# A hybrid attention and recurrence block: ScalarE, VectorE and SyncE of the input projection in program order, with each split, store and gate a set number of products behind what it needs

## The chip, the cores and the metric

The kernel runs on one core of a Trainium2 chip. The metric is the device time of one launch in microseconds, less is better. The kernel before took 2325.84 us in the median of three runs (2323.38 to 2326.81). TensorE is the matmul engine, ScalarE and VectorE work on one element per lane and cycle streams, GpSimd does general work, and SyncE only starts transfers; GpSimd starts some too. Every engine has its own queue.

## The reference

One layer of a decoder on 2048 tokens of width 1024. A sandwich-normed mixer is followed by a sandwich-normed MLP of hidden width 4096. Cut to the mixer, in which the change lies:

```python
h = rms_norm(x, mix_norm_pre)
z = h @ w_in                                   # 1024 -> 2560
q, k, v, xr, gr = split(z)                     # 512 columns each
attn = dilated_attention(q, k, v)              # 8 heads of 64, windows 128, 512, 2048, dilations 1, 4, 16
xr   = causal_depthwise_conv(xr, conv_w, conv_b)               # 4 taps
r, i = sigmoid(blocks(xr) @ w_r + b_r), sigmoid(blocks(xr) @ w_i + b_i)
a    = exp(-8 * r * softplus(-lam))
state_t = a_t * state_{t-1} + sqrt(1 - a_t ** 2) * (i_t * xr_t)
m    = concat(attn, state * gelu(gr)) @ w_out
x    = x + rms_norm(m, mix_norm_post)          # then the MLP
```

## The kernel before

**Numbers.** A float32 operand is split into an upper part, rounded by a ScalarE copy, and a lower part, the rest, by a subtraction on VectorE or GpSimd (`split`, L50). A matmul of two such operands is three: upper by upper, lower by upper, upper by lower (L206 to L208).

**Tiles of the projection.** Weights of `w_in` come in 20 tiles of 128 columns: 4 each for q, k, v, x (the recurrence's input) and g (its gate). Tokens come in blocks of 512; two blocks are a half, and a half's two blocks are b = 0 and 1. One product (`product`) is one tile by one block: 8 steps of three matmuls into one bank of PSUM. Banks have tags: "P" two buffers (products), "X" one (transposes of v, gate matmuls `pr` and `pi`, norm spreads), the others for attention.

**Stages.** `begin` opens with the products of x0, g0, x1, g1 on half 0. Then `stream` runs through the list `JOBS`, tile by tile, with both blocks of a tile. After ten products' worth of steps (`AHEADJOBS`) `interleave` takes over: it writes the attention of half 0 and between its parts calls `fill(n)`, which lets `stream` go on by n steps. So the rest of half 0's tiles and all of half 1's are computed inside and behind the attention of half 0. After that come the output projection and MLP of half 0, with the attention of half 1 in between, and those of half 1.

**What follows a product.** q and k: an eviction with the norm factor (`zn`, L219, L221), a split into `zh`, `zl`, stores to DRAM (L228, L229). v: an eviction, four transposes on TensorE (L235), a split into `vs` (one buffer), one store (L239). x: `convolved` (eviction `xr` L374, taps L377 to L380), then `opened` 10 steps later: gate matmuls `pr` (L391) and `pi` (L398), tanh, exp, square, root, and the scan of the state (L411). g: `gated`, a tanh GELU, and at its end the product with the state (L437) and a store. Weight tiles are loaded one tile ahead (`load_w`, L104) and split at once. Blocks 2 and 3 of the input replace 0 and 1 in the middle of the list (`load_x`: one transfer, an upper part `hH` L166 and a lower part `hL` L167 for each of eight column tiles; `spread_norm`: the norm's factors spread to all partitions by a matmul `pbc` L186). `between` also starts copies of `w_out` and `w2` from DRAM to DRAM on GpSimd's queue (L1550).

**What sets the order.** A step calls `passed`, which runs what `after(n, fn)` put n steps later, so the program says how many steps behind its product a thing is written. In the projection and in the attention of half 0, though, only TensorE keeps the order of the program (`manual_schedule` with PE alone). The order of ScalarE, VectorE, GpSimd and SyncE is made by a scheduler from its own estimate of times. In the attention of half 1 the order of ScalarE, VectorE and SyncE is the program's too. In the join of the heads, `sa` (L729) is made on VectorE and `pst` (L736) reads it on TensorE after one `yield`, which is one fill.

Of the kernel before, what the change touches and what calls it, by code (L numbers as in the profile page):

```python
# [86 lines left out]
class Project:  # L87
# [9 lines left out]
    def load_w(self, hf, ct, lo_eng=None, px=None):  # L97
# [3 lines left out]
        for half in range(2):  # L101
# [3 lines left out]
            split(nc, hi[:, k0:k0 + KT // 2, :], lo[:, k0:k0 + KT // 2, :], raw, lo_eng=lo_eng or self.lo)  # L105
# [39 lines left out]
    def load_x(self, tb, px=None, also=None):  # L145
# [3 lines left out]
        row = []  # L149
        b = tb % NBH  # L150
        for k in range(KT):
# [5 lines left out]
            elif px:  # L157
                raw = px.tile([P, TB], F32, tag="xl", bufs=2, name=f"xr{tb}_{k}")
            else:
                raw = self.pa.tile([P, TB], F32, tag="wraw", bufs=2, name=f"xr{tb}_{k}")  # L160
            nc.sync.dma_start(out=raw, in_=self.xT[k, :, cs])
            if tb == 0 and k == 0:
                nc.sync.dma_start(out=self.g1, in_=self.g1_d)
            hi = p.tile([P, TB], F32R, tag="hH", bufs=2 * KT, name=f"hH{tb}_{k}")
            lo = p.tile([P, TB], F32R, tag=f"hL{b}_{k}", bufs=1, name=f"hL{tb}_{k}")
            nc.scalar.activation(out=hi, in_=raw, func=AF.Identity, scale=self.g1[:, k:k + 1])  # L166
            nc.vector.scalar_tensor_tensor(out=lo, in0=raw, scalar=self.g1[:, k:k + 1], in1=f32(hi),  # L167
                                           op0=ALU.mult, op1=ALU.subtract)
            row.append((hi, lo))
            if also:  # L170
                also(k)
        self.h[tb % NBH] = row

    def spread_norm(self, tb, px=None):
# [15 lines left out]
        for j in range(TB // P):  # L190
            if px:
                made(j)
                spread(j)
            else:
                self.after(4 + 3 * j, lambda j=j: made(j))
                self.after(6 + 3 * j, lambda j=j: spread(j))
# [14 lines left out]
    def stored(self, kind, hf, pr, b, z):  # L211
# [10 lines left out]
        if kind != "v":  # L222
            zh = self.pa.tile([P, TB], F32R, tag="zh", bufs=1, name=f"zh{n}")
            zl = self.pa.tile([P, TB], F32R, tag="zl", bufs=1, name=f"zl{n}")
            self.cst["pool"] = split(nc, zh, zl, zn, lo_eng=self.lo)[1]
            dst = scr[kind][hf][pr]
            for u in range(2):
                nc.sync.dma_start(out=f32(dst[u, 0, :, cs]), in_=f32(zh[u * HD:(u + 1) * HD, :]))  # L228
                nc.sync.dma_start(out=f32(dst[u, 1, :, cs]), in_=f32(zl[u * HD:(u + 1) * HD, :]))  # L229
            return  # L230

        def turned():
            pt = self.bank("X", f"vt{n}")
            for j in range(TB // P):
# [3 lines left out]
            split(nc, vs[:, :, :, 0, :], vs[:, :, :, 1, :], ptv)  # L238
            nc.sync.dma_start(out=f32(scr["v"][hf][pr][cs, :].rearrange("(n p) c -> p n c", p=P)),  # L239
                              in_=f32(vs.rearrange("p n u a c -> p n (u a c)")))  # L240

        self.after(4, turned)

    def after(self, n, fn):

        self.due.append([n, fn])

# [8 lines left out]
    def stream(self, jobs, between):  # L256
# [5 lines left out]
        loaded = {}  # L262
# [6 lines left out]
        load()  # L269
# [97 lines left out]
    def convolved(self, hf, c, b, zx, wait, px=None):  # L367
# [7 lines left out]
        s.copy(out=self.tail[:, c, :], in_=xr[:, TB:TB + 3])  # L375
# [1333 lines left out]
```

## Time and profile before

| what | value |
|---|---|
| median of the runs | 2325.84 us (2323.38 to 2326.81) |
| the profiled execution, and its span | 2326.59 us, 2324.7 us |
| mean granted TensorE clock | 0.982 |
| TensorE busy | 2191.8 us, 94% |
| opening: 0 to 90 us | TensorE busy 79.06 |
| stream alone: 90 to 250 us | TensorE busy 147.9 of 160 |
| attention of half 0 with the rest of the stream: 250 to 555 us | TensorE busy 278.89 of 305 |
| rest of the stream: 555 to 651 us | TensorE busy 92.83 of 96 |

The times are of one execution under the profiler. A row of the timeline reads: start, duration, engine, line, operation, output, inputs, count, and in square brackets how long the engine had been idle and what ended that. A window row reads: stretch, its length, busy time (and count) of TensorE, its weight loads, VectorE, ScalarE and GpSimd, then the granted clock, the share of the DMA engines and GB/s.

### The profile page before, as it was taken

How to read it: one execution, taken by the hardware profiler on the slowest of the kernel's cores; microseconds unless marked ns; L12 is line 12 of the kernel's file. 1: busy time of each engine (PE TensorE's matmuls, PEld its weight loads, DVE VectorE, ACT ScalarE, POOL GpSimd, SP SyncE). 2: the span in 40 equal slices, each digit the busy share in tenths (PEclk: the TensorE clock that was granted, in tenths of full speed). 3: DMA queues.
4: the chain of work that ended last, by engine and by line, in shares of the span. 5: the costliest groups of instructions: out<-in, count | busy, mean ns of one | idle time of the engine just before them, and what ended most of it. 6: DMA issues, size and time to landing. Idle time of an engine off the chain costs nothing.

```text
span 2324.7 us, 30774 instructions
## 1 busy us (share of the span) xinstructions
PE 2191.8 (94%) x10264; PEld 1778.9 (77%) x10264; DVE 1510.7 (65%) x3022; ACT 1268.2 (55%) x2569; POOL 404.5 (17%) x491
## 2 busy tenths in 40 slices
PE   8989899999999899998999999898999999999998
PEld 6668677777788677786777787677878888788887
DVE  6564677685448777774667676766775656455556
ACT  7654556675334545453656565755455555563543
POOL 3434413233014201001001011114200000000003
PEclk9999999999999999999999999999999999999999
DMA  8487574424744577868767777858455443586665
GB/s 287 140 238 238 195 219 131 136 78 119 244 150 162 202 274 262 307 236 269 229 193 211 204 226 205 220 173 262 152 180 186 150 150 143 211 279 191 194 195 181
DMA packets 217551, 466.15 MB, mean 201 GB/s; under 512 B 22464, under 2 KB 77152, under 8 KB 211120
## 3 DMA queue, kind: packets, MB, share of 16 engines
q1 hardware_dynamic: 188624, 329.52, 45.3%
q0 software_dynamic: 28768, 134.66, 16.3%
q8 instruction: 81, 1.33, 0.2%
q14 instruction: 78, 0.64, 0.1%
HBM read 329.75 MB, written 151.13 MB: 207 GB/s over the span
## 4 chain that ended last, share of the span: by engine, by line
PE 49%; DVE 12%; DMA 8%; ACT 7%; issue 6%; POOL 1%; SPq 0%; DVEq 0%; ACTq 0%; POOLq 0%
PE o L1220 6%; PE o L1221 5%; PE o L1219 5%; PE za L1080 4%; PE za L1081 4%; PE za L1082 4%; PE m L906 2%; PE m L904 2%; PE m L905 2%; PE zc L1080 2%; PE zc L1081 2%; PE zc L1082 2%; DMA w2s<-in_dram 2%; PE z L206 1%; PE z L207 1%
## 5 line engine op out<-in xcount | busy, mean ns | idle before, releaser
L206 PE MATMUL z<-hH,wH 128*128 128x512 f32 x640 | 272.8, 426 | 14.8 <-DVE xr L374 7.7
L207 PE MATMUL z<-hL,wH 128*128 128x512 f32 x640 | 256.3, 400 | 0.2 <-DVE hL L167 0.2
L208 PE MATMUL z<-hH,wL 128*128 128x512 f32 x640 | 254.9, 398 | 0.0
L206 PEld LDWEIGHTS z<-hH,wH 128*128 128x128 f32 x640 | 123.3, 193 | 42.8 <-issue 13.0
L207 PEld LDWEIGHTS z<-hL,wH 128*128 128x128 f32 x640 | 122.8, 192 | 28.1 <-issue 5.1
L208 PEld LDWEIGHTS z<-hH,wL 128*128 128x128 f32 x640 | 122.5, 191 | 28.1
L514 ACT ACTIVATE smB<-smB,negB 128x128 f32<-128x128 f32 (+3 forms) x128 | 71.5, 559 | 105.2 <-DVE negB L510 104.8
L55 POOL TENSOR_TENSOR wL<-wraw,wH 128x512 fp32r<-128x512 f32 x62 | 88.8, 1449 | 171.4 <-ACT wH L54 168.7
L1085 ACT ACTIVATE sq<-sq 128x512 f32<-128x512 f32 x93 | 58.9, 633 | 84.6 <-DVE sq L1089 84.6
L514 ACT ACTIVATE sm<-sm,neg 128x256 f32<-128x256 f32 (+1 forms) x128 | 63.2, 495 | 67.9 <-DVE neg L510 67.5
L1145 POOL DMA_DIRECT2D sa<-sq x31 | 16.5, 532 | 401.3 <-ACT sq L1086 400.9
L55 DVE TENSOR_TENSOR tlB<-pT_B,thB 128x384 fp32r<-128x384 f32 x96 | 57.3, 597 | 44.2 <-ACT thB L54 43.9
L1086 ACT ACTIVATE sq<-sq 128x512 f32<-128x512 f32 x124 | 76.7, 629 | 2.4
L503 DVE CUSTOM_DVE_ANT_0 smB<-SB,mask_b 128x128 f32<-128x128 f32 (+3 forms) x128 | 59.5, 483 | 25.5 <-PE SB L679 25.4
L54 ACT CAST wH<-wraw 128x512 fp32r<-128x512 f32 (+1 forms) x81 | 46.9, 610 | 35.6 <-PE z L207 21.3
L1156 DVE TENSOR_TENSOR w2s<-w2s 128x512 f32<-128x512 f32 x64 | 44.1, 689 | 32.5 <-DMA w2s<-in_dram 31.6
L704 PE MATMUL oB<-tlB,vb 128*128 128x256 f32 x192 | 47.0, 294 | 12.6 <-DVE tlB L55 10.7
L1080 PE MATMUL za<-hHT,f_6H 128*128 128x512 f32 x128 | 51.8, 405 | 7.3 <-ACT sq L1119 7.2
L1253 POOL TENSOR_TENSOR y<-y,g4b 128x512 f32<-128x512 f32 x8 | 13.0, 1658 | 261.0 <-ACT junk_y L84 261.0
L476 PE MATMUL pT_B<-ident,smB 128*128 128x128 f32 x320 | 52.3, 278 | 5.6 <-DVE nb L497 3.6
L55 DVE TENSOR_TENSOR tlA<-pT,thA 128x512 fp32r<-128x512 f32 (+1 forms) x64 | 42.8, 668 | 22.7 <-ACT thA L54 22.2
L54 ACT CAST thB<-pT_B 128x384 fp32r<-128x384 f32 x96 | 48.5, 505 | 12.6 <-PE pT_B L476 11.9
(573 smaller groups left out, 7059.3 us busy)
## 6 DMA issues: line engine op xcount, KB each, us to landing
sa<-as POOLq DMA_DIRECT2D x32, 1024.0 KB, 5.8
w1r<-in_dram SPq DMA_DIRECT2D x58, 512.0 KB, 4.0
sa<-sq POOLq DMA_DIRECT2D x31, 768.0 KB, 3.6
wraw<-in_dram SPq DMA_DIRECT2D x79, 256.0 KB, 3.3
w2s<-in_dram SPq DMA_DIRECT2D x16, 1024.0 KB, 7.4
sb<-w2s POOLq DMA_DIRECT2D x16, 1024.0 KB, 6.5
kh<-sk SPq DMA_DIRECT2D x24, 512.0 KB, 5.1
kl<-sk SPq DMA_DIRECT2D x24, 512.0 KB, 6.6
```

The source lines that it names most:

```text
L54: return (nc.scalar.copy(out=hi, in_=src), (lo_eng or nc.vector).tensor_tensor(out=lo, in0=src, in1=f32(hi), op=ALU.subtract))
L55: (lo_eng or nc.vector).tensor_tensor(out=lo, in0=src, in1=f32(hi), op=ALU.subtract))
L206: pe.matmul(z, hi[:, k, :], hh, start=(k == 0), stop=False)
L207: pe.matmul(z, hi[:, k, :], hl, start=False, stop=False)
L208: pe.matmul(z, lo[:, k, :], hh, start=False, stop=(k == KT - 1))
L514: s.activation(out=sm[:, c0:c0 + w], in_=sm[:, c0:c0 + w], func=AF.Exp, bias=neg[:, j:j + 1], accum_out=st[:, 1, u, cols[j]:cols[j] + 1])
L1080: pe.matmul(o, hi[:, k], bh[:, k], start=start and k == 0, stop=False, skip_group_check=True)
L1081: pe.matmul(o, hi[:, k], bl[:, k], start=False, stop=False, skip_group_check=True)
L1082: pe.matmul(o, lo[:, k], bh[:, k], start=False, stop=k == KH - 1, skip_group_check=True)
L1219: pe.matmul(o, ah[:, ts], bh, start=fresh and j == 0, stop=False, skip_group_check=True)
L1220: pe.matmul(o, ah[:, ts], bl, start=False, stop=False, skip_group_check=True)
L1221: pe.matmul(o, al[:, ts], bh, start=False, stop=j == NJ - 1, skip_group_check=True)
```

## The change

Around the projection and the attention of half 0, the order of ScalarE, VectorE and SyncE is now the program's as well (`ORDERED`); GpSimd stays with the scheduler. So that the program's order can serve, each thing that follows a product is put at a number of steps of its own:

- weight tiles: cast 8 and 9 steps behind the load, the lower part one step behind each cast (before: at once);
- q and k: split at 1 and 2, upper part stored at 2, lower at 4; v: transposes at 6 (before 4), split 1 and 2 steps behind, store at 4;
- x columns of blocks 2 and 3: transfers from step k // 2, upper part of column k at 5 + k, lower at 6 + k; the norm's factors at 8 + j and 9 + j (before 4 + 3j and 6 + 3j);
- the convolution's taps at 1, sums at 3; behind `pr` the second gate at 3, weights 5, root 6, state 8, with `pi` in a "P" bank; the GELU at 1, 2, 3, 5, its end at 6;
- copies: one with each product, none with q0, k0, v0 of half 0 (before: one and then two with each call once a first split had been made);
- k3 and v3, x0 and q0 are jobs of their own; 9 products instead of 10 ahead of the attention, 24 fills instead of 16 for its first loads, gaps (1, 1, 0, 3, 4, 3) for (1, 1, 1, 3, 4, 3), and one fill ahead of each transpose group and one behind it;
- the second value load of half 0 is written after the first value products; the joins get one more `yield`, in half 1 too; `w_out` of half 0 is split 14 and 16 steps behind its load.

The core of the diff:

```diff
-            split(nc, hi[:, k0:k0 + KT // 2, :], lo[:, k0:k0 + KT // 2, :], raw, lo_eng=lo_eng or self.lo)
+            args = hi[:, k0:k0 + KT // 2, :], lo[:, k0:k0 + KT // 2, :], raw, lo_eng or self.lo
+            if px or now:
+                split(nc, *args)
+            else:
+                self.split_later(8 + half, *args)
...
+                for n, fn in ((k // 2 if k < KT - SH else 6, load), (5 + k, upper), (6 + k, lower)):
+                    self.after(n, lambda k=k, fn=fn: fn(k))
...
-            self.cst["pool"] = split(nc, zh, zl, zn, lo_eng=self.lo)[1]
+            self.split_later(1, zh, zl, zn, self.lo)
+            self.after(2, lambda: store(0, zh))
+            self.after(4, lambda: store(1, zl))
...
-        self.after(4, turned)
+        self.after(6, turned)
...
+    def split_later(self, n, hi, lo, src, lo_eng=None):
+        def lower():
+            ins = (lo_eng or self.nc.vector).tensor_tensor(out=lo, in0=src, in1=f32(hi), op=ALU.subtract)
+            if lo_eng is self.nc.gpsimd:
+                self.cst["pool"] = ins
+
+        self.after(n, lambda: self.nc.scalar.copy(out=hi, in_=src))
+        self.after(n + 1, lower)
...
+        gate_r()
+        for wait, fn in ((3, gate_i), (5, weight), (6, root), (8, state)):
+            if px:
+                fn()
+            else:
+                self.after(wait, fn)
...
-        if (hf, c, b) in self.open:
+        if (hf, c, b) in self.open and px:
             self.open[hf, c, b] = ends
         else:
-            self.after(5, ends)
+            self.after(6, ends)
...
         yield
+        yield
         pst = bank("o", f"pst{hf}_{pr}")
...
-                    for dst, src in copies[:1 if len(copies) > 2 * NJ else 2]:
-                        nc.gpsimd.dma_start(out=dst, in_=src)
-                del copies[:1 if len(copies) > 2 * NJ else 2]
+                if copies and (hf, kind, i) not in NOCOPY:
+                    with tc.issue_after(cst["pool"].ins):
+                        nc.gpsimd.dma_start(out=copies[0][0], in_=copies[0][1])
+                    del copies[0]
...
-            with tc.manual_schedule(engines={mybir.EngineType.PE}):
-                steps = pj.stream(JOBS, between)
+            with tc.manual_schedule(engines=ORDERED):
+                steps = pj.stream(JOBS, first_w, between)
...
-                               16, (1, 1, 1, 3, 4, 3), 10)
+                               24, (1, 1, 0, 3, 4, 3), 10)
...
+ORDERED = {getattr(mybir.EngineType, e) for e in ("PE", "Activation", "DVE", "SP")}
```

VectorE at the end of the opening, before. `xc_1_1`, `i_1_1`, `th_1_1` are the state chain of x tile 1 on block 1, `ge` its gates, `zn_k_0` and `zn_k_1` the evictions of k's first tile for blocks 0 and 1:

```order
L437 SCALAR_TENSOR_TENSOR ge_0_1_738<-ge_0_1_738,xc_0_1_716 128x512
L221 TENSOR_TENSOR zn_k_0_1027<-z_4_0_981,bc_585 128x512
L409 SCALAR_TENSOR_TENSOR i_1_1_1012<-i_1_1_1012,xc_1_1_814 128x512
L407 SCALAR_TENSOR_TENSOR th_1_1_1014<-a_1_1_1017,th_1_1_1014 128x512
L410 TENSOR_TENSOR i_1_1_1012<-i_1_1_1012,th_1_1_1014 128x512
L221 TENSOR_TENSOR zn_k_1_1063<-z_4_1_1038,bc_697 128x512
L411 SCALAR_TENSOR_TENSOR xc_1_1_814<-r_1_1_1008,state,i_1_1_1012 128x512
```

The same place on VectorE in the changed kernel, where `lt` and `li` are the names of `th` and `i`:

```order
L496 SCALAR_TENSOR_TENSOR ge_0_1_748<-ge_0_1_748,xc_0_1_725 128x512
L454 SCALAR_TENSOR_TENSOR lt_1_1_1004<-la_1_1_1005,lt_1_1_1004 128x512
L455 SCALAR_TENSOR_TENSOR li_1_1_1003<-li_1_1_1003,xc_1_1_823 128x512
L461 TENSOR_TENSOR li_1_1_1003<-li_1_1_1003,lt_1_1_1004 128x512
L462 SCALAR_TENSOR_TENSOR xc_1_1_823<-lr_1_1_1002,state,li_1_1_1003 128x512
L463 COPY state<-xc_1_1_823 128x1
L496 SCALAR_TENSOR_TENSOR ge_1_1_831<-ge_1_1_831,xc_1_1_823 128x512
L241 TENSOR_TENSOR zn_k_0_1022<-z_4_0_969,bc_595 128x512
L241 TENSOR_TENSOR zn_k_1_1060<-z_4_1_1026,bc_707 128x512
```

The two k evictions stood before and within the chain, and now stand behind all of it.

GpSimd's queue around the first v store, before. `swo` and `sw` are targets of the copies, `wL` lower parts of weight tiles, `zl` those of k:

```order
L55 TENSOR_TENSOR wL_14_1074<-wraw_14_1_1079,wH_14_1073 128x512
L55 TENSOR_TENSOR zl_k_1_1066<-zn_k_1_1063,zh_k_1_1065 128x512
L1550 DMA swo_207<-in_dram 16x8192
L1550 DMA swo_200<-in_dram 16x8192
L1550 DMA swo_201<-in_dram 16x8192
L1550 DMA swo_202<-in_dram 16x8192
L1550 DMA swo_203<-in_dram 16x8192
L1550 DMA sw_168<-in_dram 128x512
L1550 DMA sw_168<-in_dram 128x1024
```

The same queue in the changed kernel, from the same lower part of k on:

```order
L274 TENSOR_TENSOR zl_k_1_1063<-zn_k_1_1060,zh_k_1_1062 128x512
L274 TENSOR_TENSOR wL_14_1065<-wraw_14_0_1066,wH_14_1064 128x512
L274 TENSOR_TENSOR wL_14_1065<-wraw_14_1_1068,wH_14_1064 128x512
L1623 DMA swo_204<-in_dram 16x8192
L1623 DMA swo_205<-in_dram 16x8192
L274 TENSOR_TENSOR wL_18_1143<-wraw_18_0_1144,wH_18_1142 128x512
L274 TENSOR_TENSOR wL_18_1143<-wraw_18_1_1146,wH_18_1142 128x512
L1623 DMA swo_206<-in_dram 16x8192
L1623 DMA swo_207<-in_dram 16x8192
```

A row of copies has become two copies between the splits of one weight tile and the next.

ScalarE where the columns of block 2 are made, before. `hH` are upper parts of columns, `pT` and `thB` softmax tiles on their way back from the transposes, `fold` attention outputs:

```order
L166 ACTIVATE hH_0_3132<-xr_0_3130,g_sb 128x512
L166 ACTIVATE hH_1_3138<-xr_1_3136,g_sb 128x512
L166 ACTIVATE hH_2_3144<-xr_2_3142,g_sb 128x512
L496 COPY fold<-oA_3_1_3106 64x512
L166 ACTIVATE hH_3_3150<-xr_3_3148,g_sb 128x512
L166 ACTIVATE hH_4_3156<-xr_4_3154,g_sb 128x512
```

The same columns in the changed kernel:

```order
L173 ACTIVATE hH_0_3241<-xr_0_3189,g_sb 128x512
L173 ACTIVATE hH_1_3254<-xr_1_3191,g_sb 128x512
L173 ACTIVATE hH_2_3265<-xr_2_3193,g_sb 128x512
L278 CAST vs_v_0_3252<-vt_v_0_3247 128x8x64
L173 ACTIVATE hH_3_3288<-xr_3_3195,g_sb 128x512
L54 CAST thB_3296<-pT_B_3_3_0_3298 128x384
L173 ACTIVATE hH_4_3317<-xr_4_3201,g_sb 128x512
```

From the third column on, each stands alone between casts of the attention and of v.

More of the change, by code (lines that the diff above doesn't have):

```diff
@@ L148, in load_x, with load @@
         cs = slice(tb * TB, (tb + 1) * TB)
-        row = []
+        row = self.h[tb % NBH] = []
         b = tb % NBH
-        for k in range(KT):
+        raws = {}
+        def load(k):
             if k < KT - SH:
@@ L194, in spread_norm @@
             else:
[L195 to L196 removed]
+                self.after(8 + j, lambda j=j: made(j))
+                self.after(9 + j, lambda j=j: spread(j))
         self.bc[tb % NBH] = bcast
@@ L827, in split_there, with load_w_out @@
     split(nc, hi, lo, f32(lo), lo_eng)
-def load_w_out(tc, p, w_out, hf, order, cst, between):
+def load_w_out(tc, p, w_out, hf, order, cst, between, later=None):
     nc = tc.nc
```

188 lines of the change are left out of this document (110 added, 78 removed).

## The prediction

> **What bounds the kernel now.** The page comes first, then the projection by stage, then the waits of TensorE inside each stage.
>
> ```profile
> PE 2191.8 (94%) x10264; PEld 1778.9 (77%) x10264; DVE 1510.7 (65%) x3022; ACT 1268.2 (55%) x2569; POOL 404.5 (17%) x491
> ...
> PE   8989899999999899998999999898999999999998
> ```
>
> TensorE is busy for 94% of the span. No other engine passes 65%. The change adds and removes no matmul, so all it can win or lose is idle time of TensorE and the slow stretches that follow it. The windows by stage say how much of that there is (span, then busy us and instructions of PE, PEld, DVE, ACT, POOL; PEclk; DMA share; GB/s):
>
> ```profile
> 90.00:160.00 70.00, 57.93 (x236) 43.78 (x235) 38.31 (x49) 32.81 (x50) 27.38 (x31) 0.93 0.81 238
> 160.00:250.00 90.00, 90.00 (x513) 76.57 (x512) 44.30 (x132) 41.42 (x116) 36.88 (x45) 1.00 0.83 268
> 250.00:555.00 305.00, 278.89 (x1428) 223.49 (x1427) 228.22 (x519) 208.12 (x457) 93.75 (x76) 0.97 0.42 129
> ...
> 1110.00:1545.00 435.00, 400.51 (x2171) 330.57 (x2169) 305.01 (x762) 271.01 (x611) 37.75 (x68) 0.99 0.69 203
> ```
>
> From 160 to 250 us nothing can be won: TensorE has no gap. From 90 to 160 it idles 12.1 us, in the attention of half 0 (250 to 555) 26.1. The last row, the attention of half 1, is the yardstick: there ScalarE, VectorE and SyncE already stand in program order, and 34.5 us of 435 are idle, or 7.9 in 100. Half 0 under the scheduler has 8.6 in 100. **Program order by itself is thus no cure**; what counts is which single waits the new distances remove.
>
> **The change, part by part.** The counts of matmuls, casts and evictions stay; what moves is when they stand. A step is three matmuls of a product.
>
> *(a) The first v store.* A timeline of all engines around it:
>
> ```profile
> 106.42 2.43 POOL L1550 DMA_DIRECT2D swo<-in_dram  x5
> ...
> 107.69 0.55 SPq L239 DMA_DIRECT2D sv<-vs_v  x1
> ...
> 108.84 1.58 POOL L1550 DMA_DIRECT2D sw<-in_dram  x3
> ...
> 125.89 0.58 ACT L54 CAST vs_v<-vt_v 128x512 fp32r<-128x512 f32 x1 [15.91 <-DMA sv<-vs_v]
> ...
> 127.11 1.05 DVE L374 TENSOR_TENSOR xr<-z,bc 128x512 f32<-128x512 f32 x1
> ...
> 128.31 0.77 PE L206 MATMUL z<-hH,wH 128*128 128x512 f32 x1 [7.73 <-DVE xr L374]
> ```
>
> ```profile
> L239 SPq DMA_DIRECT2D sv<-vs_v x16: 377/382/603, 107.7 to 658.1; - x16
> ...
> DMA to landing us min/median/max: 2.9/4.1/18.1
> ```
>
> Eight copies go out around the store of the first v block, and that store lands 18.1 us after its issue, where the median is 4.1. The staging buffer `vs` is single, so the cast of the second block stands 15.91 us on ScalarE, its VectorE half behind it, and behind that in VectorE's queue the eviction L374, for which TensorE waits 7.73 us. By the changed order no copy goes out for q0, k0 and v0, then one for each product. At the median landing the buffer is free at 107.7 + 4.1 = 111.8, 14 us before the cast that now waits for it, so the 7.7 us go, and with them most of the small waits of the same chain. I take −9.0: of 12.1 idle us, 2.5 belong to (d), leaving 9.6, of which I keep 0.5. Behind the gap TensorE runs at half rate (rows under b): −1.5 more. **−10.5** (ends 0, if the copies still delay the store, and −11).
>
> ScalarE, VectorE and GpSimd take their queues strictly in order, says the Trainium skill ("PSUM — Partial Sum Buffer", section "Engine vs sequencer instructions"). This trace agrees, with 15.91 us on the cast and an eviction behind it. The rule speaks against the change as much as for it: an order fixed in advance puts the next late transfer ahead of an eviction in the same way; that is the slower rival below.
>
> *(b) The waits in the attention of half 0.* TensorE's timeline, its gaps of 2 us and more:
>
> ```profile
> 256.68 2.08 PE L391 MATMUL pr<-xc,bd_r 128*128 128x512 f32 x2 [3.17 <-DVE xc L380]
> ...
> 288.66 0.39 PE L704 MATMUL oB<-tlB,vb 128*128 128x256 f32 x1 [2.03 <-DVE tlB L55]
> ...
> 325.44 0.49 PE L186 MATMUL pbc<-dg,ones 128*128 128x128 f32 x2 [2.06 <-DVE vs_v L55]
> ...
> 345.12 0.80 PE L186 MATMUL pbc<-dg,ones 128*128 128x128 f32 x2 [2.71 <-DVE vs_v L55]
> ...
> 369.83 0.39 PE L645 MATMUL oA<-tlA,va 128*128 128x256 f32 x1 [2.60 <-DVE tlA L55]
> ...
> 443.00 0.66 PE L235 MATMUL vt_v<-ident,zn_v 128*128 128x128 f32 x4 [2.44 <-ACT r L394]
> 444.35 0.63 PE L207 MATMUL z<-hL,wH 128*128 128x512 f32 x1
> 444.78 0.63 PE L208 MATMUL z<-hH,wL 128*128 128x512 f32 x1
> ...
> 448.33 0.39 PE L207 MATMUL z<-hL,wH 128*128 128x512 f32 x1
> 448.56 0.40 PE L208 MATMUL z<-hH,wL 128*128 128x512 f32 x1
> ```
>
> The six sum to 15.0 us. Each is one matmul that reaches TensorE before a VectorE or ScalarE result that the scheduler had put behind other work: the sums of a convolution, transposes whose bank a late tanh still held, a norm's spread behind v splits, a softmax's lower half. The change names a distance for these: sums and gate 3 and 10 steps behind the product, transposes at 6 instead of 4, the spread at 9. I take **−15**, with the other 11.1 us left as they are. The ends: −26.1 if none is left, and −2 if half 0 becomes as dense in gaps as the yardstick (7.93 × 3.05 = 24.2 us left).
>
> *(c) The half rate behind those gaps.* The 444 rows are 0.43 us apart, the 448 rows 0.23. It lasts from 444 to 447, so one such gap costs about 1.4 us more. In the window the granted clock is 0.97, so at most 0.03 × 305 = 9.2 us are there. Six gaps would give 8.4; **−6**, as the small gaps left keep some (ends 0 and −9.2). The Trainium skill ("TensorE: Matmul & The Clock Gate", section "Why this matters for your kernels") lets throughput fall only behind idle gaps of over some 3 us. The trace differs: the gap at 443.00 has 2.44 us and half rate behind it. By that rule only the gap at 256.68 would count, term c would be near −1.5, and the sum 2299.
>
> *(d) A new wait at the end of the opening.* The state chain of pair (1,1) now stands whole ahead of the first k eviction on VectorE, and ahead of the k cast on ScalarE.
>
> ```profile
> 85.33 2.04 PE L391 MATMUL pr<-xc,bd_r 128*128 128x512 f32 x2 [2.99 <-DVE xc L380]
> ...
> 93.07 0.68 DVE L221 TENSOR_TENSOR zn_k<-z,bc 128x512 f32<-128x512 f32 x1
> 93.83 0.62 ACT L54 CAST zh_k<-zn_k 128x512 fp32r<-128x512 f32 x1 [3.86 <-DVE zn_k L221]
> 94.36 0.68 ACT L394 ACTIVATE r<-pr,vec_br 128x512 f32<-128x512 f32 x1
> 94.37 0.40 PE L206 MATMUL z<-hH,wH 128*128 128x512 f32 x1
> ...
> 101.21 0.50 PE L206 MATMUL z<-hH,wH 128*128 128x512 f32 x1 [1.16 <-DVE zn_k L221]
> ...
> 102.96 1.90 DVE L437 SCALAR_TENSOR_TENSOR ge<-ge,xc 128x512 f32<-128x512 f32 x1
> ...
> 105.61 0.63 PE L235 MATMUL vt_v<-ident,zn_v 128*128 128x128 f32 x4 [1.36 <-DVE zn_v L221]
> ```
>
> The chain ran from 94.36 to 104.86, 10.5 us, with one k eviction (0.68) between: 9.8 alone. In the new order ScalarE can begin it where it stood idle, at 93.83 − 3.86 = 89.97. It ends at 99.8, the eviction behind it at 100.4, and the product that TensorE reached at 94.37 waits for that bank: 6.1 us. That replaces the gaps of 1.16 and 1.36, so +3.6, and +1.4 for half rate: **+5**. Behind the eviction wait the k cast, its two stores on SyncE and the v eviction. Ends: +1 if the chain begins when its gate matmuls end (87.4), +9.4 if it begins no sooner than now.
>
> *(e) The x columns of blocks 2 and 3.*
>
> ```profile
> L166 ACT ACTIVATE hH<-xr,g_sb x16: 710/722/730, 317.0 to 351.6; 128x512 fp32r<-128x512 f32 x16
> ```
>
> ```profile
> L167 DVE SCALAR_TENSOR_TENSOR hL<-xr,g_sb,hH x16: 740/750/1826, 317.8 to 354.2; 128x512 fp32r<-128x512 f32 x16
> ```
>
> Sixteen columns were made over 35 us; now one falls to each step of two successive products. The steps of a stage are counted by the first matmul of each:
>
> ```profile
> 250.00:555.00 305.00, 113.79 (x260) 50.43 (x260) 0.97 0.42 129
> 90.00:651.00 561.00, 233.60 (x550) 105.62 (x550) 0.97 0.58 178
> ```
>
> A step lasts 305/260 = 1.17 us in the attention, so 16 last 18.8. ScalarE has 16 × 0.72 = 11.6 us for them, beside its other load of (208.1 − 11.6)/305 × 18.8 = 12.1: 23.7 us of work in 18.8, 4.9 over. VectorE: 16 × 0.75 = 12.0 and (228.2 − 12.0)/305 × 18.8 = 13.3, 6.5 over. Stored blocks and free banks hide part of that. **+4** (ends 0 and +6.5).
>
> *(f) The tail.*
>
> ```profile
> 618.11 1.11 PE L235 MATMUL vt_v<-ident,zn_v 128*128 128x128 f32 x4 [3.17 <-DVE zn_v L221]
> ```
>
> The transposes of v stand two steps later (1.4 us) and nothing moves ahead of the eviction that they need: **−4** with its half rate (ends 0 and −4.6).
>
> *(g) One fill more before the joins' matmuls*, in half 1 too:
>
> ```profile
> PE pst L736 <- DVE sa L729: 5.3, 4, 1.4
> ```
>
> One fill is longer than 1.4 us of matmuls in all but the last: **−4.5** (ends 0 and −5.3).
>
> Costed at nothing: the value loads of half 0 that move behind the first value products, the weights of the output projection at set distances, the shorter pauses in the order of fills. What hides them is the queue of products on TensorE. Without that cover each costs a transfer of a few us, once per head or once in all.
>
> **Sum:** −10.5 − 15 − 6 + 5 + 4 − 4 − 4.5 = −31. The profiled execution took 2326.59 us (span 2324.7), 0.75 above the median of the runs, 2325.84. 2326.6 − 31 − 0.75 gives **2295 us**. All good ends together: −11 − 26.1 − 9.2 + 1 − 4.6 − 5.3 = −55.2, 2271. All bad ones: −2 + 9.4 + 6.5 = +13.9, 2340.
>
> **The rivals.**
>
> *All waits go.* Every ordered wait in the attention has its distance, and (d) and (e) are hidden: 2271. For it speaks 160 to 250 us, without a gap already; against it the yardstick, 8% idle in program order.
>
> *Waits are exchanged.* The named gaps go, but as many new ones come, as in the yardstick: b is −2, c is −1, the sum −13: 2313. For it speaks that a softmax of half 0 shares ScalarE with evictions just as in half 1.
>
> *The copies aren't spread.* GpSimd is still left to the scheduler; if it puts copies beside the v store again, (a) is 0: 2306. Against it stands the new order, with two copies between splits where nine stood in a row.
>
> *A wash.* b −2, c 0, f 0, (d) and (e) at their bad ends: −10.5 − 2 + 9.4 + 6.5 − 4.5 = −1, 2325.
>
> *Slower: a late weight block holds ScalarE.* The cast now stands eight steps behind the issue of its load, ahead of casts and softmax in a fixed order.
>
> ```profile
> L104 SPq DMA_DIRECT2D wraw<-in_dram x78: 327/346/9570, 7.9 to 622.0; - x78
> ...
> DMA to landing us min/median/max: 2.5/3.3/8.5
> ```
>
> From 90 to 651 us a step lasts 561/550 = 1.02, so the cast comes 8.2 us behind. A block that lands later stops ScalarE and then TensorE. Forty copies, one to a product, stand beside 20 tiles. At landings of L this costs 20 × (L − 8.2): at 10.7 it is 50, 2345; it outweighs the gain from 9.8 us on. Against it: median 3.3, maximum 8.5, and the copies are thinner than before. For it: the v store did take 18.1.
>
> **How the numbers follow.** Forecast 0.47, all waits go 0.12, exchanged 0.19, copies not spread 0.04, wash 0.06, slower 0.12. A measurement of this kernel can tell about 0.2% (4.7 us) from no change: faster 0.82, within 0.2% 0.06, slower 0.12. The range leaves out the wash and the slower case, 18 in 100, and reaches to the others with 3 us more below and 9 above the exchange: 2268 to 2322.
>
> **What would show it.** (a) The first v store lands in 3 to 5 us and no wait over 2 us stands before L374's successor; (b) in the attention of half 0 TensorE idles near 11 us, not 24; (c) its clock there is 0.99; (d) a gap of about 6 us near 95 us, released by the k eviction; (e) new waits on columns where block 2 is first used; (f, g) no gap of 3 us in the tail, no wait on `sa` but the last. A wait of ScalarE on weight blocks beyond 13 us in all would make the forecast wrong.

## The result: slower by 1.2%, and where the time went

The changed kernel took 2352.5 us in the median (2346.5 to 2361.2) against 2325.9 before: a ratio of 1.0119, with a 95% interval of 1.0085 to 1.0153. Forecast were 2295 us and a range of 2268 to 2322.

The page of the changed kernel, as before busy time by engine and TensorE's busy tenths:

```profile
PE 2208.4 (94%) x10264; PEld 1792.4 (76%) x10264; DVE 1517.2 (64%) x3025; ACT 1269.1 (54%) x2569; POOL 393.4 (17%) x488
...
PE   8899888898999999999898999898999999999998
```

It does the same work. TensorE's busy time grew by 16.6 us for as many matmuls, since more of them ran at half rate (the granted clock from 90 to 680 us is 0.94, before 0.97); the rest of the 27.9 us by which the span grew is idle time. To see where, both executions are cut at the same events: TensorE's first score matmul, the last value product of half 0's attention (oB), the first matmul of the output projection, the end. Before:

```profile
0.00:158.60 158.60, 135.59 (x528) 99.88 (x529) 96.52 (x156) 107.43 (x172) 56.13 (x77) 0.96 0.69 219
158.60:547.80 389.20, 363.10 (x1915) 295.41 (x1914) 270.34 (x650) 248.98 (x571) 129.92 (x120) 0.97 0.52 162
547.80:650.80 103.00, 99.83 (x452) 81.02 (x452) 46.78 (x73) 30.69 (x54) 20.36 (x17) 0.98 0.66 198
650.80:2324.70 1673.90, 1593.32 (x7373) 1302.56 (x7372) 1097.01 (x2144) 881.13 (x1772) 198.07 (x278) 0.99 0.63 208
```

And after:

```profile
0.00:158.30 158.30, 138.19 (x528) 102.92 (x529) 93.48 (x155) 107.58 (x171) 50.95 (x70) 0.94 0.57 186
158.30:571.10 412.80, 368.39 (x1887) 296.83 (x1886) 272.66 (x640) 241.36 (x562) 125.97 (x124) 0.95 0.52 164
571.10:688.20 117.10, 108.92 (x479) 87.65 (x479) 54.25 (x87) 38.34 (x65) 19.56 (x17) 0.96 0.60 180
688.20:2352.60 1664.40, 1592.93 (x7373) 1304.99 (x7371) 1096.80 (x2145) 881.78 (x1772) 196.94 (x278) 0.98 0.63 209
```

The opening is even (−0.3 us), the attention 23.6 us longer, the tail 14.1, all behind it 9.5 shorter: +27.9. The attention holds 28 matmuls fewer than before and the tail 27 more at 0.23 us each, so like for like the loss is about 30 in the attention and 8 in the tail. Its idle time rose from 26.1 to 44.4.

TensorE's timeline of the changed kernel, its gaps of over 2.3 us from 90 us on:

```profile
100.62 0.77 PE L226 MATMUL z<-hH,wH 128*128 128x512 f32 x1 [6.99 <-DVE zn_k L241]
...
144.35 0.80 PE L226 MATMUL z<-hH,wH 128*128 128x512 f32 x1 [3.24 <-ACT li L446]
...
276.50 0.39 PE L769 MATMUL oB<-thB,vb 128*128 128x256 f32 x1 [4.71 <-ACT thB L54]
...
324.29 0.33 PE L535 MATMUL pT_B<-ident,smB 128*128 128x128 f32 x1 [3.42 <-ACT smB L573]
...
350.73 0.46 PE L206 MATMUL pbc<-dg,ones 128*128 128x128 f32 x2 [2.66 <-DVE vs_v L274]
...
385.73 0.40 PE L707 MATMUL oA<-thA,va 128*128 128x256 f32 x1 [3.50 <-ACT thA L54]
...
444.37 0.58 PE L769 MATMUL oB<-thB,vb 128*128 128x256 f32 x1 [2.39 <-ACT thB L54]
447.70 0.58 PE L769 MATMUL oB<-tlB,vb 128*128 128x256 f32 x1 [2.75 <-DVE tlB L55]
...
584.34 0.58 PE L802 MATMUL pst<-sel,sa 128*16 128x32 f32 x8 [3.56 <-DVE sa L794]
...
605.82 0.79 PE L226 MATMUL z<-hH,wH 128*128 128x512 f32 x1 [3.90 <-ACT wH L278]
```

The gaps named in the forecast are mostly gone, and others stand in their place: six of these ten behind a cast, a tanh or an exponential of ScalarE that came late, four behind VectorE. What ScalarE waited for in the stretch from 90 to 690 us (total, times, longest), its largest wait and the larger ones on transfers:

```profile
ACT vs_v L278 <- PE vt_v L259: 34.1, 9, 8.7
ACT wH L278 <- DMA wraw<-in_dram: 30.0, 9, 12.8
...
ACT zh_k L278 <- DMA sk<-zh_k: 15.5, 4, 6.2
...
ACT ge L485 <- DMA smix<-ge: 13.3, 4, 4.1
...
ACT zh_q L278 <- DMA sq<-zh_q: 9.9, 2, 6.5
```

All waits of ScalarE on transfers sum to 76.6 us here. Before, they were 67.0 from 90 to 651 us (an expectation below says 32; v stores alone make 28.3 of the 67). In the attention alone they rose from 24.6 to 33.9.

One of these waits, followed back, in the timeline of all engines:

```profile
310.99 0.62 ACT L278 CAST zh_k<-zn_k 128x512 fp32r<-128x512 f32 x1 [2.20 <-POOL wL L274]
...
314.98 5.09 SPq L627 DMA_DIRECT2D va<-sv  x8
...
320.17 1.13 SPq L249 DMA_DIRECT2D sk<-zh_k  x2
...
323.23 0.62 ACT L278 CAST zh_k<-zn_k 128x512 fp32r<-128x512 f32 x1 [6.21 <-DMA sk<-zh_k]
323.75 0.40 ACT L573 ACTIVATE smB<-smB,negB 128x128 f32<-128x128 f32 x1
...
324.29 0.33 PE L535 MATMUL pT_B<-ident,smB 128*128 128x128 f32 x1 [3.42 <-ACT smB L573]
```

SyncE's longest wait from 285 to 326 us:

```profile
SPq L627 <- PE oA L707: 16.2, 1, 16.2
```

The upper part of the last k block is ready at 311.6 us. SyncE, in program order, stands for 16.2 us before the eight small value loads, until TensorE at 314.95 has read the one buffer that they fill, and then issues them, 5.1 us. The k store stands behind them and goes out at 320.17, 8.6 us after its data were ready. The next k cast needs that store's buffer and stands 6.2 us on ScalarE; behind it in the fixed order stands an exponential whose inputs are there since 321.1 at the latest, and TensorE waits for it. The gap at 276.50 has another root of the same form: ScalarE's tanh of block 1 waits 6.03 us for VectorE's scan of block 0, and the cast `thB` stands behind the tanh. VectorE was late there itself: ahead of the scan its tiny `negB` (128x2) took 2.72 us from 269.36 on, where others of its form take 0.17, while GpSimd made three subtractions (268.28 to 272.04). Why it took so long, no run isolates. ScalarE's rows:

```profile
274.09 1.28 ACT L439 ACT_TABLE_LOAD   x1 [6.03 <-DVE xc L462]
...
275.97 0.47 ACT L54 CAST thB<-pT_B 128x384 fp32r<-128x384 f32 x1
```

### The profile page after: what moved, and what is told of

Same layout as the page of the kernel before. It is cut to its first block, busy times and chain, and to the rows that moved or that the text cites. A ratio compares the mean times of both kernels' runs of the same rounds, so it can differ in the third digit from the quotient of the medians.

```text
span 2352.6 us, 30715 instructions
## 1 busy us (share of the span) xinstructions
PE 2208.4 (94%) x10264; PEld 1792.4 (76%) x10264; DVE 1517.2 (64%) x3025; ACT 1269.1 (54%) x2569; POOL 393.4 (17%) x488
## 3 DMA queue, kind: packets, MB, share of 16 engines
q0 software_dynamic: 28768, 134.66, 16.1%
## 4 chain that ended last, share of the span: by engine, by line
PE 57%; DVE 14%; DMA 9%; ACT 9%; issue 6%; POOL 1%; SPq 1%; ACTq 0%; DVEq 0%; POOLq 0%
PE o L1289 6%; PE o L1288 6%; PE o L1290 6%; PE za L1149 4%; PE za L1150 4%; PE za L1151 4%; PE z L226 3%; PE z L227 3%; PE z L228 3%; PE zc L1149 2%; PE zc L1150 2%; PE zc L1151 2%; PE m L973 2%; PE m L975 2%; PE m L974 2%
## 5 line engine op out<-in xcount | busy, mean ns | idle before, releaser
L226 PE MATMUL z<-hH,wH 128*128 128x512 f32 x640 | 278.8, 436 | 24.1 <-ACT li L446 7.4
L227 PE MATMUL z<-hL,wH 128*128 128x512 f32 x640 | 261.2, 408 | 0.8 <-DVE hL L178 0.8
L227 PEld LDWEIGHTS z<-hL,wH 128*128 128x128 f32 x640 | 126.3, 197 | 29.3 <-issue 4.6
L228 PEld LDWEIGHTS z<-hH,wL 128*128 128x128 f32 x640 | 125.5, 196 | 29.3 <-DVE wL L274 0.2
L274 POOL TENSOR_TENSOR wL<-wraw,wH 128x512 fp32r<-128x512 f32 x56 | 76.0, 1370 | 185.4 <-ACT wH L278 164.7
L769 PE MATMUL oB<-thB,vb 128*128 128x256 f32 x192 | 48.7, 277 | 18.0 <-ACT thB L54 15.5
L278 ACT CAST wH<-wraw 128x512 fp32r<-128x512 f32 x70 | 42.1, 617 | 30.3 <-DMA wraw<-in_dram 30.0
```

Source lines behind the costliest of these rows:

```text
L226: pe.matmul(z, hi[:, k, :], hh, start=(k == 0), stop=False)
L227: pe.matmul(z, hi[:, k, :], hl, start=False, stop=False)
L228: pe.matmul(z, lo[:, k, :], hh, start=False, stop=(k == KT - 1))
L769: pe.matmul(dst.rearrange("p (i m) -> p i m", m=P), vb[:, x * NC + c, :], t[:, cols].rearrange("p (i m) -> p i m", m=P)[:, ::step], start= ...
```

## The experiments

All times are medians; beside each run the kernel before ran on the same chip (medians of 2321.6 to 2326.0 us, so that between groups of runs some 4 us are the chip's). "In order" is the program's order, "free" the scheduler's.

### Which part costs: the distances, or the order?

**The distances without the order.** Only TensorE in order, everything else of the change kept.

```diff
-            with tc.manual_schedule(engines=ORDERED):
+            with tc.manual_schedule(engines={mybir.EngineType.PE}):
```

> The changed kernel with all its distances, but only TensorE in program order; ScalarE, VectorE and SyncE are left to the scheduler again. Theory A (the fixed order is what costs: ScalarE waits 72 us for transfers against 32 before, and VectorE 39 us for folds against 3): 2310 to 2325 us. Theory C (the distances, the pauses and TensorE's own new order cost): 2345 or more, as the changed kernel, 2352.

Measured: 2305.7 us, ratio 0.9916 (0.99 to 0.9932). **The change has two parts of opposite sign**: its distances gain 18 us, its fixed order costs 47. Theory C is out. The stages of this run, cut as above:

```profile
0.00:152.50 152.50, 134.38 (x528) 100.47 (x529) 93.52 (x156) 107.29 (x172) 51.69 (x70) 0.98 0.65 211
152.50:534.60 382.10, 359.06 (x1888) 291.91 (x1887) 265.92 (x641) 240.26 (x561) 127.12 (x124) 0.97 0.53 170
534.60:645.00 110.40, 106.58 (x480) 85.93 (x480) 56.29 (x85) 37.91 (x65) 21.50 (x17) 0.98 0.63 191
645.00:2306.80 1661.80, 1593.45 (x7373) 1306.20 (x7371) 1096.69 (x2145) 881.85 (x1772) 197.21 (x278) 0.98 0.64 209
```

Against before, the opening gains 6.1 us and the part behind the projection 12.1; attention and tail together are even (492.5 against 492.2). Most of those 12.1 come with the second `yield` of the joins alone: the run that has only this edit, the last below, takes 1663.8 us for that part. Against the changed kernel, the order alone adds 5.8 in the opening, 30.7 in the attention, 6.7 in the tail and 2.6 behind it. The same matmuls of the attention cost 9.3 us more of busy time (half rate) and 21.4 more of idle time.

**Whose order?** The same edit with other sets of engines.

> The changed kernel with SyncE alone given back to the scheduler. Theory B (SyncE's fixed order holds stores and weight loads behind waits of the attention's transfers, and ScalarE then waits for those): ScalarE's waits on DMAs fall from 72 us to near 32, 2320 to 2330 us. Theory A (ScalarE and VectorE hold each other): 2345 to 2355.

> The changed kernel with ScalarE alone given back to the scheduler; VectorE and SyncE stay in program order. If ScalarE's order is the cost (it stands 72 us before late transfers and VectorE behind it): 2305 to 2320 us, as with only TensorE ordered (2306). If VectorE's order is the cost: 2345 to 2360. If the two hold each other, each alone gives about half: 2325 to 2335.

> The changed kernel with VectorE alone given back to the scheduler; ScalarE and SyncE stay in program order. If VectorE's order is the cost (39 us before folds of ScalarE, gate sums and scans behind softmax pieces): 2305 to 2320 us. If ScalarE's order is the cost: 2345 to 2360. If the two hold each other: 2325 to 2335.

> The changed kernel with TensorE and SyncE in program order, ScalarE and VectorE with the scheduler. If SyncE's order costs nothing of its own (as giving it back alone gained nothing): 2304 to 2311 us, as with TensorE alone ordered (2306). If the weight blocks that it loads late (ScalarE waits 30 us for them in the changed kernel) cost TensorE: 2318 to 2330.

> TensorE and ScalarE in program order, VectorE and SyncE with the scheduler. If ScalarE's order is the one that costs beside SyncE's: 2325 to 2340 us. If it takes ScalarE and VectorE together: 2306 to 2315.

> TensorE and VectorE in program order, ScalarE and SyncE with the scheduler. ScalarE's order alone cost 27 us over TensorE's alone and SyncE's 32. If any fixed order beside TensorE's costs this much: 2328 to 2342 us. If VectorE's order does no harm of its own: 2304 to 2312.

| in order beside TensorE | us | ratio to before, 95% | to first score | attention | tail |
|---|---|---|---|---|---|
| none | 2305.7 | 0.9916 (0.99 to 0.9932) | 152.5 | 382.1 | 110.4 |
| SyncE | 2338.2 | 1.0058 (1.0034 to 1.0082) | 155.3 | 403.2 | 115.1 |
| ScalarE | 2332.3 | 1.0034 (1.002 to 1.0048) | 155.0 | 398.2 | 114.3 |
| VectorE | 2334.3 | 1.0052 (1.0034 to 1.007) | 161.1 | 385.2 | 120.6 |
| VectorE, SyncE | 2339.4 | 1.007 (1.0042 to 1.0098) | 152.7 | 407.2 | 116.8 |
| ScalarE, SyncE | 2335.2 | 1.0058 (1.0036 to 1.0081) | 156.7 | 393.8 | 113.0 |
| ScalarE, VectorE | 2359.8 | 1.0151 (1.0133 to 1.0169) | 163.4 | 408.5 | 120.8 |
| all three | 2352.5 | 1.0119 (1.0085 to 1.0153) | 158.3 | 412.8 | 117.1 |

No single engine is the culprit: each one alone in order costs 27 to 32 us. The costs of ScalarE and VectorE add (54 us together), but every set with SyncE in it costs far less than the sum of its members. Only the expectations for ScalarE and VectorE alone in order hold; the other four measured times lie outside all of their ranges, by 0.2 to 8 us. SyncE's and ScalarE's order cost in the attention (21 and 16 us), VectorE's in the opening and the tail (9 and 10). Giving SyncE back alone made ScalarE's waits on weight blocks vanish from the list altogether, but its waits on transfers stayed, 79.5 us, now with v stores first (27.8), and so did the time: **late weight blocks are not what the whole costs**. Theory B as stated is out, though SyncE's order by itself is harmful. How, the timeline shows in the run with SyncE alone in order:

```profile
576.50 2.39 SPq L831 DMA_DIRECT2D co<-sco  x4
...
582.64 2.36 SPq L831 DMA_DIRECT2D co<-sco  x4
585.04 1.12 SPq L104 DMA_DIRECT2D wraw<-in_dram  x2
...
590.38 1.21 ACT L278 CAST wH<-wraw 128x512 fp32r<-128x512 f32 x2 [14.30 <-DMA wraw<-in_dram]
...
591.05 0.79 PE L226 MATMUL z<-hH,wH 128*128 128x512 f32 x1 [7.10 <-ACT wH L278]
```

Eight small loads of a join hold SyncE for 8.5 us: four are issued, then SyncE stands for 3.75 us until GpSimd at 582.61 has read their one buffer, then come the other four. The weight block of the next tile is issued behind them, and TensorE stands 7.1 us. With only TensorE in order, the scheduler put stores into the same pause, and had issued a weight block ahead of the loads:

```profile
553.42 2.39 SPq L831 DMA_DIRECT2D co<-sco  x4
555.91 1.18 SPq L249 DMA_DIRECT2D sq<-zh_q  x2
...
559.97 2.38 SPq L831 DMA_DIRECT2D co<-sco  x4
```

### Does the order cost at a few places that can be mended?

**The folds** (copy and sum of an attention output one fill later):

```diff
-        s.copy(out=t, in_=o[HD:P, :])
-        v.tensor_tensor(out=dst, in0=o[0:HD, :].rearrange(pat, **kw), in1=t.rearrange(pat, **kw), op=ALU.add)
+        def turned():
+            s.copy(out=t, in_=o[HD:P, :])
+            v.tensor_tensor(out=dst, in0=o[0:HD, :].rearrange(pat, **kw), in1=t.rearrange(pat, **kw), op=ALU.add)
+
+        if hf:
+            turned()
+        else:
+            FOLDS.append(turned)
...
+            while i == 0 and FOLDS:
+                FOLDS.pop(0)()
```

> The changed kernel, all four engines in order; in half 0 the copy and the sum of an attention output (fold) are written one fill later, not right behind the matmuls that they read. VectorE waited 39 us there for ScalarE's copy, and ScalarE 20 us for those matmuls, with casts and evictions of the stream behind both. If the order holds the engines at these places: 2330 to 2342 us and VectorE's waits on folds under 15 us. If they are only where a lag from elsewhere shows: 2348 to 2358.

Measured: 2354.0, ratio 1.0128 (1.01 to 1.0156). No gain, though VectorE's waits on folds fell from 39 to 21 us. The folds are where a lag from elsewhere shows.

**The scan ahead of the next tanh:**

```diff
-        for wait, fn in ((3, gate_i), (5, weight), (6, root), (8, state)):
+        for wait, fn in ((3, gate_i), (5, weight), (6, root), (7, state)):
```

> The changed kernel with the scan of the state 7 instead of 8 steps behind its gate, so that it stands ahead of the next block's first tanh, which writes the tile that the scan reads. If this order costs what the trace shows (ScalarE 14.5 us before scans, one gap of TensorE of 4.7 us behind it): 2342 to 2348 us. If the wait is covered or only moves: 2349 to 2356.

Measured: 2350.1, ratio 1.0115 (1.0087 to 1.0142), no difference. The gap at 276 us shrank from 4.71 to 4.20: VectorE itself came late to the scan, since the product ahead of it (L461) took 4.20 us, where the median of this line is 0.69.

**The first k eviction ahead of the state chain of pair (1,1):**

```diff
-        followed(1, 1, 24)
+        followed(1, 1, 26)
```

> The changed kernel, all four in order, with the gates of pair (1,1) 26 instead of 24 steps behind their product, so that the first k eviction stands ahead of the state chain on VectorE. The forecast's term (d) by itself: the gap of 7.0 us at 100 us goes and the attention begins 5 to 8 us sooner, 2344 to 2348 us. If the chain's wait moves to the next eviction: 2350 to 2356.

Measured: 2350.7, ratio 1.0103 (1.0081 to 1.0126). The opening got 3.3 us shorter (155.0 against 158.3), but waits of 4.3 and 2.9 us on the evictions of q and k took the place of 7.0 on the first of k. The chain's wait mostly moves, as the rival said; in the median no difference can be told.

**Eights of transfers off SyncE**, to GpSimd's queue (`g`) as in half 1, for SyncE alone in order and for all. The edit takes both off SyncE, the issuing and the waits for the buffers:

```diff
-                (g if hf else nc.sync).dma_start(out=f32(va[cs, hf + 4 * i:hf + 4 * i + 4, :]),
+                g.dma_start(out=f32(va[cs, hf + 4 * i:hf + 4 * i + 4, :]),
...
-        dma = (g if hf else nc.sync).dma_start
+        dma = g.dma_start
```

> TensorE and SyncE in program order, as in the run that took 2338 us, but the small transfers that come in eights (the value tiles va, and the joins' sco and co) issued on GpSimd's queue in half 0 too, as they are in half 1. If SyncE's order costs because these eights (5.1 and 8.5 us of issuing) stand ahead of weight blocks and stores: 2306 to 2320 us, no wait of TensorE on a weight block of 7 us. If it costs because its waits stand in a fixed order: 2332 to 2342.

Measured: 2350.1, ratio 1.0113 (1.0089 to 1.0138): worse than without the edit (2338.2). The run doesn't decide its question. TensorE's wait on the weight's upper part went, but one of 5.7 us on its lower part came, and the joins on GpSimd finished later, so that the value products waited 23.2 us for `nb`, which has one buffer (7.0 without the edit):

```profile
PE oB L769 <- DVE nb L556: 23.2, 3, 9.4
```

> The changed kernel, all four in order, with the same transfers on GpSimd's queue and nothing else. If the eights on SyncE are the first cause of the late casts (zh_k at 323, wH at 442): 2335 to 2345 us. If ScalarE and VectorE hold each other without them: 2348 to 2358.

Measured: 2338.8, ratio 1.0054 (1.0037 to 1.0071): 14 us gained, as expected if the eights on SyncE, with the waits before them, are a first cause; 7.5 of them in the attention (405.3 us).

**All named places at once**: the eights off SyncE and the scan at 7, as above, and

```diff
-                self.split_later(8 + half, *args)
+                self.split_later(12 + half, *args)
...
-        r, i, th, a2 = [p.tile([P, TB], F32, tag=t, bufs=1, name=f"{t}{n}") for t in ("lr", "li", "lt", "la")]
+        r, i, th, a2 = [p.tile([P, TB], F32, tag=t, bufs=1, name=f"{t}{n}") for t in (("la", "li", "lt", "lr") if b and not px else ("lr", "li", "lt", "la"))]
```

> All four in order, and slack at each place where the trace shows ScalarE held: the eights on GpSimd's queue, weight casts 12 instead of 8 steps behind the load, the scan at 7, and the first tanh of block 1 into the tile of the square, so that it doesn't wait for block 0's scan. If these named places are the cause of the order's cost in the attention (31 us above the run with TensorE alone in order): 2318 to 2332 us. If the order has no few places, and each removed wait only bares the next: 2340 to 2352.

Measured: 2341.8, ratio 1.0068 (1.0044 to 1.0093), no better than the eights alone. The attention still lasts 407.9 us, against 412.8 unrepaired and 382.1 with the order free:

```profile
156.10:564.00 407.90, 367.86 (x1888) 296.04 (x1887) 271.04 (x642) 240.74 (x565) 159.10 (x180) 0.95 0.51 165
```

**ScalarE's places alone**, with only TensorE and ScalarE in order and no transfer moved (weight casts at 12, the scan at 7 and the tanh's tile, without the eights):

> TensorE and ScalarE in program order (2332 us), with slack at ScalarE's named places: weight casts 12 steps behind the load, the scan at 7, the first tanh of block 1 into the tile of the square. No transfer is moved, so GpSimd's queue stays as it is. If these places are what ScalarE's order costs: 2308 to 2318 us. If the order costs at places that shift with each repair: 2324 to 2338.

Measured: 2325.6, ratio 0.9999 (0.9984 to 1.0015). Some 7 us are won back of the 27 that ScalarE's order costs; in the attention, 392.8 us now, 5.4 of 16.1.

### Is it slack against TensorE?

Fills are steps of the stream between the parts of the attention; more of them give each cast more time, and leave fewer for the tail. The second part of the edit runs what is still due when the stream ends.

```diff
-                               24, (1, 1, 0, 3, 4, 3), 10)
+                               24, (1, 1, 0, 5, 6, 5), 10)
...
+                while pj.due:
+                    pj.passed()
```

> The changed kernel, all four in order, with two fills more between the transposes and the value products of each attention part: (1, 1, 0, 5, 6, 5) for (1, 1, 0, 3, 4, 3); the steps come out of the rest of the stream behind the attention. If the order costs because TensorE comes for a cast only a few steps behind it, with ScalarE and VectorE 65 to 75% busy (no slack): 2322 to 2338 us. If the engines hold each other whatever TensorE does: 2345 to 2358.

Measured: 2357.3, ratio 1.0142 (1.0114 to 1.017). The time can't be told from the changed kernel's. In the profiled execution, which at 2367.75 us lies above the median, attention and tail together took 523.4 us instead of 529.9, so that slack gained at most 6.5 of the 37 that the order costs there, and new waits of 7.35, 4.56 and 4.20 us come from the gates. The part behind lost 20.7 us; 12.0 of them, TensorE's wait for a `w_out` block, show that the emptied tail no longer hides its splits.

> The same two fills more, with only TensorE in program order (2306 us without them). If slack is what TensorE's waits lack there too: 2292 to 2302 us. If the scheduler already places the casts as well as can be: 2304 to 2312.

Measured: 2312.9, ratio 0.9949 (0.9934 to 0.9964): worse than 2305.7. The tail is down to 47.9 us, with TensorE busy for 37.8 of them.

> One fill more, (1, 1, 0, 4, 5, 4), with only TensorE in program order: between 2306 us and the run with two fills more, if each fill takes its share of the waits; else 2304 to 2312.

Measured, with (1, 1, 0, 4, 5, 4) in the same edit: **2296.9, ratio 0.9897 (0.9864 to 0.993)**, the lowest median of all runs, below both of its ranges, and faster than both kernels. Against the same kernel without the extra fill (0.99 to 0.9932) the intervals overlap, so that a gain by the fill is not shown. In the profiled executions attention and tail together last 480.6 us against 492.5:

```profile
150.10:558.00 407.90, 387.18 (x2036) 317.46 (x2035) 281.04 (x656) 253.46 (x580) 140.13 (x136) 0.98 0.54 169
558.00:630.70 72.70, 71.33 (x333) 57.62 (x332) 36.11 (x59) 25.09 (x46) 20.14 (x15) 1.00 0.74 228
```

### The join by itself

The second `yield` put into the kernel before, and nothing else:

```diff
         yield
+        yield
         pst = bank("o", f"pst{hf}_{pr}")
```

> The kernel before with one edit of the change: the second yield ahead of the joins' last matmuls. The forecast's term (g): 4 to 5 us less than before, 2319 to 2322, TensorE's wait on sa gone from the attention of half 1. If the wait only moves to another place there: 2324 to 2328.

Measured: 2315.5 us, ratio 0.9968 (0.9952 to 0.9984), and the wait on `sa` fell from 5.3 us to 0.4. That is more than forecast; what gains the rest was not traced.

## Why the prediction was wrong

**The step that failed** is the one in (b): "I take −15, with the other 11.1 us left as they are", with a bad end of −2 from the yardstick of half 1. Measured: idle time there rose by 18 us (26.1 to 44.4) instead of falling by 15, and with the half rate of (c) the attention lost 30 us like for like. The working treated the six gaps as faults of single places that new distances remove, and the order itself as free, because half 1 is in order and has no more gaps per us than half 0 under the scheduler. The runs show that the fixed order of the other engines costs 47 us here, 31 of them in the attention, and that the distances without it change attention and tail by nothing (492.5 against 492.2): idle time fell by 2.4 us (29.3 to 26.9), and busy time rose by as much. The yardstick was no bound, either. In half 1 the value loads and the joins' transfers go out on GpSimd's queue, and `nb` has two buffers; in half 0 they stand on SyncE among stores and weight blocks, and the yardstick's row didn't show that. Moving these transfers won back 14 of the 47 us.

**Point by point.** (a) was right in what it removes: the store no longer holds the next cast, no transfer of v takes over 7.8 us, the 7.73 us gap is gone. Its gain was eaten by (d), 7.0 us against the 6.1 worked out, and by a wait that no term had: 3.2 us at 144 for the tanh `li`, which must have read the "P" bank of `pi` before the next product can use it. The gaps that went (7.73, 1.16, 1.36) and those that came (6.99, 3.24) sum to 10.2 us each. So the opening is even instead of 5.5 us shorter. (c) fell with (b): the granted clock of the attention went from 0.97 to 0.95, not to 0.99. (e): TensorE waited 0.8 us for columns of x in all, and 3.4 for norm spreads (4.8 before); no cost of 4 us shows there. (f) was wrong: the 3.17 us on `zn_v` went, and 3.9 us on a weight cast came. (g) was right in its mechanism and too small: 6.1 us by medians for the join alone, and 10.1 in its part behind the projection (1663.8 against 1673.9); but in the last join of half 0 the changed kernel waits 3.56 us for `sa`, where the forecast had none.

**The rivals.** The slower one came nearest. It said that in a fixed order a late transfer holds ScalarE, and ScalarE then TensorE; the traces show just that. But it named late landing, and the point of 9.8 us was never reached: weight blocks landed in 4.6 us in the median and 8.3 at most. They were issued late, behind eights of small transfers and the waits for their buffers. ScalarE's waits on weight blocks, 30.0 us, passed the 13 that the forecast gave as the sign of being wrong; yet with SyncE free, when ScalarE waited for no weight block, ScalarE's and VectorE's order cost as much by other waits. One mechanism with one price was too narrow a rival for a change that removes a scheduler's freedom from three engines.

**What stays open.** Why each engine alone costs more than half as much as all three, and why SyncE's cost doesn't add to the others', was not settled. GpSimd stayed with the scheduler in every run. The repairs show that a part, at most 14 us, sits at nameable places; the rest moved when a place was mended. That it is head-of-line waiting in general, and not some place not yet found, is argued, not shown. The run with SyncE alone in order and no eights was spoilt by `nb`'s single buffer; a second buffer was not tried.

## What to carry to other kernels

An order written by hand and the distances in it are two changes: try the distances with the scheduler's order first, which here (the joins' second `yield` included) is the whole gain, and price the loss of each engine's freedom before taking it. A stage that runs well in program order is a yardstick for another only if its queues carry the same transfers and its tiles have as many buffers. A transfer that waits for a buffer holds everything behind it on a queue in fixed order: look for such a wait ahead of each transfer that others need. Moving filler from a later stage into a crowded one can be too much: two fills more cost 7 us here (2305.7 to 2312.9), and whether one more gains (2296.9) is within the noise.

## What the hardware showed that was not expected

The half rate of TensorE doesn't follow the length of the gap. Before, the gap of 2.44 us at 443.00 had half rate behind it up to 447, and the one of 2.60 us at 369.83 none; TensorE's timeline of the kernel before:

```profile
369.83 0.39 PE L645 MATMUL oA<-tlA,va 128*128 128x256 f32 x1 [2.60 <-DVE tlA L55]
```

Where the gaps lie makes the difference. Two stretches around each, as window rows:

```profile
365.30:368.60 3.30, 1.85 (x9) 1.09 (x7) 3.21 (x10) 2.33 (x6) 1.41 (x1) 1.00 0.00 0
368.70:372.00 3.30, 2.17 (x15) 1.97 (x16) 3.30 (x6) 2.25 (x7) 2.07 (x2) 1.00 0.34 89
...
440.40:443.70 3.30, 0.86 (x7) 0.70 (x7) 1.36 (x7) 2.69 (x3) 0.00 (x0) 1.00 0.01 2
443.80:447.10 3.30, 3.30 (x12) 2.82 (x11) 1.50 (x6) 2.96 (x8) 0.00 (x0) 0.50 0.08 28
```

The shorter gap lies whole in one stretch (2.44 us idle), and the granted clock of the next is 0.50. The longer one lies across two (1.45 and 1.13 us idle), and the clock stays at 1.00. In both executions the granted clock changes only on a fixed grid of 3.41 us. Cut on that grid from 90 to 680 us, all 18 falls to half rate come behind a stretch with 1.65 to 3.18 us of idle time; where the full rate lasted on, the stretch before had at most 1.62. Over the traces of all runs the two groups overlap between 1.4 and 1.9 us, so that this is no sharp threshold.

In the changed kernel half rate came behind a gap of only 1.65 us, and not at once: 1.7 us later, for 3.4 us, which is one stretch of the grid. The rows:

```profile
370.59 0.36 PE L707 MATMUL oA<-thA,va 128*128 128x256 f32 x1 [1.65 <-ACT sm L573]
...
372.06 0.41 PE L226 MATMUL z<-hH,wH 128*128 128x512 f32 x1
372.30 0.60 PE L227 MATMUL z<-hL,wH 128*128 128x512 f32 x1
...
375.68 0.42 PE L227 MATMUL z<-hL,wH 128*128 128x512 f32 x1
```

So a price of 1.4 us for each gap, as in term (c), is no rule: of its six gaps, those at 325.44 and 369.83 had no half rate behind them, three had 3.4 us of it, and the one at 256.68 had 10.2. The Trainium skill ("TensorE: Matmul & The Clock Gate", section "Why this matters for your kernels") names gaps of over some 3 us; here gaps of 2.0 to 2.7 us, and one of 1.65, were followed by half rate. And a SyncE transfer is not free to issue: eight `co` loads took 4.75 us of its queue (8.5 with the wait between them) and eight `va` loads 5.1, while a weight block lands in 4.6 in the median.
